# Low parts of u in half-tile loads, one more stored low part, and the first half's closing additions interleaved by bank

## The chip, the cores and the metric

One core of a Trainium2 chip runs the whole kernel in one launch. The metric is device time in microseconds (us), as the median of the runs; a profiled execution gives the trace that is read here. The core has a matrix engine (PE, with its weight loads PEld), a vector engine (DVE), an activation engine (ACT), a general engine (POOL) and a sync engine (SP). SP, ACT and POOL also issue DMA transfers, each into its own queue (q1, q10 and q0 in the profile), and each engine takes its instructions strictly in order.

## What is computed

A decoder layer over 256 tokens of width 2048, in float32. The change touches only the last stage, the feed-forward block:

```python
h = _rmsnorm(x, norm_mlp_pre[layer])
u = jnp.square(jax.nn.relu(h @ w_up[layer]))               # 256 x 8192
x = x + _rmsnorm(u @ w_down[layer], norm_mlp_post[layer])  # w_down: 8192 x 2048
```

## The kernel before

**Precision.** A float32 product is made of three PE products. Each operand is split into a high part (a rounded copy, made by ACT, `hi`) and a low part (the rest, made by DVE, `lo`); the products hi·hi, lo·hi and hi·lo are added up in PSUM (`three`, line 1031). Each weight tile of 128x1024 thus comes by a DMA into `raw` (5 buffers), is split by ACT (line 306) and DVE (line 307) into `hi` and `lo`, and is then used by PE. The class `Weights` runs this up to six tiles ahead of PE.

**The up and the down product.** `w_up` is taken in 8 chunks of 1024 columns; each leaves two groups of u, `uT[0]` to `uT[15]`, transposed, 128x1024 each (four slices of 128 rows of u's inner dimension, times 256 tokens). The down product takes `w_down` in two halves of 1024 columns, `c` = 0 and 1 (the first and the second half), and runs through all 16 groups `g` of u in each. Its inner dimension counts 64 slices `k`, or 32 pairs `kp` of slices; group g covers kp = 2g and 2g+1. A pair is done either as two plain steps (4 blocks of y times 3 parts per slice: 24 PE products, 5.4 us) or, for the pairs in `DOWN_SEVEN`, as seven block products in place of eight (7 times 3 parts: 21 PE products, 4.8 us): kp = 5, 7, 9, 11, 15, 17, 19, 21, 25, 27, 29 in the first half, and 3, 5, ... 27 in the second.

**Pair loads.** A pair with seven products needs sums of weight blocks. Its two weight slices come as one transfer of 1 MB that POOL issues (line 374) into `ab_down`, `c` or `u01`, in turn; DVE then adds blocks into `st_down` (lines 361, 365, 366), and ACT and DVE split the four tiles. I call this transfer the *pair load* of kp. In DVE's order these three additions stand ahead of the splits of the plain pair before, so a late pair load holds those back too.

**The low part of u.** u is used twice, and its low part is not kept in SBUF. After a group is finished, `lo_away` writes minus its rounded copy (`neg`) to DRAM by two ACT transfers into `ukeep[g]`, and later POOL issues two transfers of 256 KB that add u to it in DRAM (line 967, `ukeep<-u`, `accum_op=OP.add`), which leaves the low part there. `split_u` fetches it by one POOL transfer of 512 KB per group (line 979, `ulo<-ukeep`) into one of two buffers, issued after the first step of the group before, and makes the high part `uhi` on ACT. Group 0 has no stored low part: DVE makes it in both halves (line 981).

**The order of work.** There is no scheduler at run time. `Flow` keeps an estimated PE clock while the program is written out; generators such as `lo_away` and `half_evac` are resumed when that clock has passed the time that their last `yield` asked for, and this fixes where their instructions stand in each engine's order. POOL's queue therefore holds, in a fixed order, `ulo` loads, pair loads, the adding transfers and the reloads of sums of u (`s<-skeep`); a `ulo` load that waits until PE has finished with its buffer stops all that stand behind it.

**Closing the first half.** After the first half, `more` (in `c`) is added to each of four PSUM banks (`y`), ACT takes the sum of squares of the bank (`square`, `junkd`), and DVE writes the bank times the gain into `c` (line 1197). `half_evac` (line 1188) does this bank by bank during the first pairs of the second half, interleaved with DVE's splits. The banks are then reused as `md` by the seven-product pairs of the second half.

Of the kernel before, what the change touches and what calls it, by code (L numbers as in the profile page):

```python
# [26 lines left out]
P = 128  # L27
# [236 lines left out]
def layer(nc, tc, io):  # L264
# [49 lines left out]
    def tok(t, k, b):  # L314
        return t[:, k, b * P:(b + 1) * P]
# [617 lines left out]
    def up_evac(j, b, i, acc, order):  # L933
# [15 lines left out]
        nc.scalar.activation(uT[j][:, :, b * P:(b + 1) * P], t.rearrange("p (k s) -> p k s", k=4), AF.Square)  # L949
        if b and j:  # L950
            flow.start(lo_away(j), 2.0 + 4.0 * (j % 2))

    def lo_away(g):

        ukeep[g] = dram.tile([P, CW], F32, name=f"ukeep{g}")
        u = uT[g].rearrange("p k s -> p (k s)")
        for h in range(2):
            c = slice(h * 512, (h + 1) * 512)
            t = late["up"].tile([P, 512], F32, tag="r", bufs=2, name=f"neg{g}_{h}")
            nc.scalar.activation(t.bitcast(F32R), u[:, c], AF.Copy, scale=-1.0)  # L960
            yield 1.0
            nc.scalar.dma_start(out=ukeep[g][:, c], in_=t)
            yield 7.0
        yield 16.0
        for h in range(2):
            c = slice(h * 512, (h + 1) * 512)
            nc.gpsimd.dma_start(out=ukeep[g][:, c], in_=u[:, c], accum_op=OP.add)
            yield 2.0

    def split_u(c, g):  # L970
        if (c, g) == (0, 0):
            uh, ul = [wp.tile([P, CW], F32R, tag=w, bufs=W_BUFS, name=f"u{w}0").rearrange("p (k s) -> p k s", k=4)
                      for w in ("hi", "lo")]
        else:
            uh, ul = [dpl["dp"].tile([P, 4, S], F32R, tag=f"u{w}", bufs=2, name=f"u{w}{c}_{g}") for w in ("hi", "lo")]
        u, h, l = [x.rearrange("p k s -> p (k s)") for x in (uT[g], uh, ul)]
        if g:
            nc.scalar.activation(h, u, AF.Copy)
            nc.gpsimd.dma_start(out=l.bitcast(F32), in_=ukeep[g])
        else:  # L980
            split(h, l, u)
        return uh, ul

# [151 lines left out]
    def down_mm(c, u, k, b, n, w, first, last):  # L1135
        three(y[b][2 * c + n], [tok(u[x], k % 4, b) for x in range(2)], [t[:, 0, n * 512:n * 512 + 512] for t in w],
              first, last)
# [50 lines left out]
    def half_evac(more, g_half):  # L1188

        for n in range(2):  # L1190
            for b in range(NB):
                tt, out = nc.vector.tensor_tensor, more[b, n]
                tt(out=y[b][n], in0=y[b][n], in1=out, op=OP.add)
                yield 1.0
                square(n, b)
                yg[n, b] = out
                tt(out=out, in0=y[b][n], in1=g_half[n], op=OP.mult)
                yield 1.0

# [12 lines left out]
    for c in range(2):  # L1212
# [5 lines left out]
        for t, (what, k, tiles) in enumerate(wide_d[c]):  # L1218
# [10 lines left out]
            else:  # L1229
                if k == ws[0]:  # L1230
# [4 lines left out]
                    m = {i: bank(4 * (1 - c) + o, f"md{i}_{c}") for o, i in enumerate((1, 6, 7, 5))}  # L1235
                blocks = [[tok(u[x], 2 * (k % 2) + kk, bb) for x in range(2)] for kk, bb in ((0, 0), (1, 0), (1, 1))]
# [22 lines left out]
    for g in (GT - 2, GT - 1):  # L1259
        for b, n in PARTS:  # L1260
            for kk in range(4):
# [4 lines left out]
                else:  # L1266
                    three_more(y[b][2 + n], [tok(us[1, g][x], kk, b) for x in range(2)],
                               [t[:, 0, n * 512:n * 512 + 512] for t in w])
# [52 lines left out]
```

## Time and profile before

| what | value |
|---|---|
| median of 3 runs | 1049.46 us (1048.84 to 1049.66) |
| profiled execution, its own time | 1049.74 us |
| its span, first to last instruction | 1047.9 us, granted PE clock 0.998 |
| PE / DVE / ACT / POOL busy | 1035.3 / 834.0 / 644.5 / 90.4 us |
| down product in the trace | 703 to 1040 us; second half from 871 us |
| HBM traffic | 222.16 MB read, 25.17 MB written |

The profiled execution lies 0.28 us above the median of the runs. A busy PE is modelled, so its idle time is read from the starts of its products: undisturbed, one starts 0.227 us after the other. In the timelines each row has the start, the duration, the engine and line, and in square brackets how long the engine idled before it and what ended that.

### The profile page before, as it was taken

Reading aid. Unit: us, or ns where it says so; the run is one execution under the profiler, and the core shown is the slowest. Engines: PE = TensorE matmul, PEld = TensorE weight load, DVE = VectorE, ACT = ScalarE, POOL = GpSimd, SP = SyncE. Lnnn points to the kernel's source line nnn. Section 1 sums busy time; section 2 is a strip of 40 time slices with the busy share of each in tenths; the row PEclk is TensorE's granted clock in tenths of the full one; section 3 lists DMA queues with packets and bytes.
Section 4 is the critical chain, followed back from the end, with each engine's and each line's share of the span. In section 5 each row is a group of like instructions: output and inputs, shape, how many; then the busy total and the mean of one; then the engine's idle time right before and its main releaser. Section 6 shows DMA issues by size and latency. Waiting matters only on the chain.

```text
span 1047.9 us, 13455 instructions
## 1 busy us (share of the span) xinstructions
PE 1035.3 (99%) x4828; PEld 860.3 (82%) x4828; DVE 834.0 (80%) x1122; ACT 644.5 (62%) x884; POOL 90.4 (9%) x134
## 2 busy tenths in 40 slices
PE   9999999999999999999999999999999999999996
PEld 6888889888888788888888888788888888788785
DVE  6676536567557669999999999796989888998895
ACT  6674436565555566675766767666757564866661
POOL 0000000000000000111101011011201001212100
PEclk9999999999999999999999999999999999999999
DMA  9975447454447295758879587589997977789862
GB/s 301 368 230 150 139 131 240 142 162 156 145 164 235 84 370 180 252 177 263 238 237 289 174 251 232 164 289 346 306 380 250 362 260 236 276 314 338 330 233 81
DMA packets 89395, 248.21 MB, mean 237 GB/s; under 512 B 7920, under 2 KB 12528, under 8 KB 88944
## 3 DMA queue, kind: packets, MB, share of 16 engines
q1 hardware_dynamic: 61984, 162.03, 45.9%
q0 software_dynamic: 22592, 77.08, 23.3%
q10 hardware_dynamic: 4752, 8.24, 2.2%
q8 instruction: 38, 0.62, 0.2%
q14 instruction: 29, 0.24, 0.1%
HBM read 222.16 MB, written 25.17 MB: 236 GB/s over the span
## 4 chain that ended last, share of the span: by engine, by line
PE 86%; DVE 6%; DMA 3%; issue 2%; ACT 2%; SPq 0%; POOL 0%; DVEq 0%; POOLq 0%; ACTq 0%
PE acc_u L296 21%; PE y L296 20%; PE acc_o L296 8%; PE m L296 6%; PE md L296 5%; PE acc_v L296 4%; PE acc_qk L296 4%; DVE lo L307 3%; PE acc_ckv L296 2%; PE acc_ukv L296 2%; PE acc_q L296 2%; PE acc_cq L296 2%; PE acc_k L296 2%; PE acc_uq L296 2%; PE rt L300 1%
## 5 line engine op out<-in xcount | busy, mean ns | idle before, releaser
L307 DVE TENSOR_TENSOR lo<-raw,hi 128x1024 fp32r<-128x1024 f32 (+3 forms) x207 | 233.5, 1149 | 81.8 <-ACT hi L306 81.1
L306 ACT ACTIVATE hi<-raw 128x1024 fp32r<-128x1024 f32 (+3 forms) x207 | 203.3, 996 | 67.4 <-DMA raw<-in_w_in 15.4
L296 PE MATMUL acc_u<-hi,hT_hi 128*128 128x512 f32 x356 | 141.7, 398 | 0.0
L296 PE MATMUL acc_u<-hi,hT_lo 128*128 128x512 f32 x356 | 139.2, 391 | 0.4 <-DVE hT_lo L307 0.4
L296 PE MATMUL acc_u<-lo,hT_hi 128*128 128x512 f32 x356 | 138.8, 390 | 0.0
L296 PE MATMUL y<-hi,ulo 128*128 128x512 f32 x352 | 137.1, 390 | 0.8 <-DMA ulo<-ukeep 0.8
L296 PE MATMUL y<-lo,uhi 128*128 128x512 f32 x352 | 137.1, 390 | 0.7 <-DVE lo L307 0.7
L296 PE MATMUL y<-hi,uhi 128*128 128x512 f32 x352 | 137.3, 390 | 0.0
L310 ACT ACTIVATE hi<-raw,gcol 128x1024 fp32r<-128x1024 f32 x74 | 83.0, 1147 | 31.9 <-DMA raw<-in_w_up 20.1
L311 DVE SCALAR_TENSOR_TENSOR lo<-raw,gcol,hi 128x1024 fp32r<-128x1024 f32 x74 | 92.4, 1278 | 11.1 <-ACT hi L310 11.0
L296 PEld LDWEIGHTS acc_u<-hi,hT_lo 128*128 128x128 f32 x356 | 66.8, 188 | 14.9 <-DVE hT_lo L307 0.8
L296 PEld LDWEIGHTS y<-hi,ulo 128*128 128x128 f32 x352 | 66.0, 188 | 15.0 <-DMA ulo<-ukeep 1.2
L296 PEld LDWEIGHTS y<-lo,uhi 128*128 128x128 f32 x352 | 66.1, 188 | 14.6 <-DVE lo L307 1.2
L296 PEld LDWEIGHTS acc_u<-lo,hT_hi 128*128 128x128 f32 x356 | 67.0, 188 | 13.0
L296 PEld LDWEIGHTS acc_u<-hi,hT_hi 128*128 128x128 f32 x356 | 66.9, 188 | 12.8
L296 PEld LDWEIGHTS y<-hi,uhi 128*128 128x128 f32 x352 | 66.1, 188 | 13.7
L306 ACT ACTIVATE hi<-u 128x1024 fp32r<-128x1024 f32 (+1 forms) x38 | 37.5, 990 | 47.6 <-DVE u L366 34.7
L307 DVE TENSOR_TENSOR lo<-st_down,hi 128x1024 fp32r<-128x1024 f32 x48 | 57.5, 1219 | 1.1 <-ACT hi L306 1.0
L296 PE MATMUL md<-hi,s 128*128 128x512 f32 x144 | 52.1, 389 | 0.0
L306 ACT ACTIVATE hi<-st_down 128x1024 fp32r<-128x1024 f32 x48 | 49.8, 1050 | 3.4 <-DVE st_down L366 2.9
L296 PE MATMUL acc_o<-hi,mixT_hi 128*128 128x512 f32 x128 | 51.8, 405 | 0.0
L296 PE MATMUL acc_o<-hi,mixT_lo 128*128 128x512 f32 x128 | 50.2, 392 | 0.0
(330 smaller groups left out, 2171.1 us busy)
## 6 DMA issues: line engine op xcount, KB each, us to landing
raw<-in_w_down SPq DMA_DIRECT2D x80, 512.0 KB, 6.1
raw<-in_w_up SPq DMA_DIRECT2D x76, 512.0 KB, 6.4
raw<-in_w_in SPq DMA_DIRECT2D x55, 512.0 KB, 5.1
ab<-in_w_up POOLq DMA_DIRECT2D x22, 1024.0 KB, 6.1
raw<-in_w_out SPq DMA_DIRECT2D x32, 512.0 KB, 4.4
ulo<-ukeep POOLq DMA_DIRECT2D x30, 512.0 KB, 6.7
ab_down<-in_w_down POOLq DMA_DIRECT2D x13, 1024.0 KB, 9.2
ukeep<-neg ACTq DMA_DIRECT2D x30, 256.0 KB, 4.4
```

What stands on the lines that cost most here:

```text
L296: nc.tensor.matmul(out, a, b, start=start, stop=stop)
L300: nc.tensor.transpose(out, a, ident)
L306: nc.scalar.activation(hi, src, AF.Copy)
L307: nc.vector.tensor_tensor(out=lo, in0=src, in1=hi.bitcast(F32), op=OP.subtract)
L310: nc.scalar.activation(hi, src, AF.Copy, scale=g)
L311: nc.vector.scalar_tensor_tensor(out=lo, in0=src, scalar=g, in1=hi.bitcast(F32), op0=OP.mult, op1=OP.subtract)
```

## The change

1. `lo_away` is started for group 0 too, so that its low part is stored; in the second half it is loaded in place of DVE's subtraction. In the first half group 0 is split on DVE as before.
2. The wait between the `neg` stores and the adding transfers is 34 us of the estimated clock in place of 16, so these stand later in POOL's order.
3. The low part is loaded in halves of 256 KB, each for one pair, into four buffers of half the size; the half for pair kp+3 is issued after pair kp is written out (a plain pair: after its first step).
4. `half_evac` writes the gain multiplication of one bank after the addition of the next one, instead of right after its own.

```diff
-        if b and j:
+        if b:
             flow.start(lo_away(j), 2.0 + 4.0 * (j % 2))
...
-        yield 16.0
+        yield 34.0
         for h in range(2):
...
+        uh = dpl["dp"].tile([P, 4, S], F32R, tag="uhi", bufs=2, name=f"uhi{c}_{g}")
+        nc.scalar.activation(uh.rearrange("p k s -> p (k s)"), uT[g].rearrange("p k s -> p (k s)"), AF.Copy)
+        load_lo(2 * (c * GT + g) + 1)
+        return uh, [u_lo.pop(2 * (c * GT + g) + h) for h in range(2)]
+
+    u_lo = {}
+    next_lo = [2]
+
+    def load_lo(upto):
+
+        for i in range(next_lo[0], min(upto + 1, 4 * GT)):
+            g, h = i // 2 % GT, i % 2
+            t = u_lo[i] = dpl["dp"].tile([P, 2, S], F32R, tag="ulo", bufs=4, name=f"ulo{i}")
+            nc.gpsimd.dma_start(out=t.rearrange("p k s -> p (k s)").bitcast(F32), in_=ukeep[g][:, h * 512:(h + 1) * 512])
+            next_lo[0] = i + 1
...
+        def half_gain(b, n):
+            yg[n, b] = more[b, n]
+            nc.vector.tensor_tensor(out=more[b, n], in0=y[b][n], in1=g_half[n], op=OP.mult)
+
+        done = []
         for n in range(2):
             for b in range(NB):
-                tt, out = nc.vector.tensor_tensor, more[b, n]
-                tt(out=y[b][n], in0=y[b][n], in1=out, op=OP.add)
+                nc.vector.tensor_tensor(out=y[b][n], in0=y[b][n], in1=more[b, n], op=OP.add)
+                square(n, b)
                 yield 1.0
-                square(n, b)
-                yg[n, b] = out
-                tt(out=out, in0=y[b][n], in1=g_half[n], op=OP.mult)
-                yield 1.0
+                if done:
+                    half_gain(*done.pop())
+                    yield 1.0
+                done.append((b, n))
+        half_gain(*done.pop())
...
+            load_lo(2 * c * GT + (k if what == "w" else k // 2) + 3)
             nxt = (c, g + 1) if g < GT - 1 else (1, 0)
```

PE's and SP's orders do not change. POOL's order at the start of the down product, before: the number behind `ukeep` and the last one of `ulo0_1` is the group; the two `ab_down` rows are the pair loads of kp 5 and 9, and the `c` row is that of kp 7.

```order
L979 DMA ulo0_1_6408<-ukeep1_3831 128x1024
L967 DMA ukeep12_6087<-ab_3502 128x512
L374 DMA ab_down_6373<-in_w_down 128x2x1024
L967 DMA ukeep12_6087<-ab_3502 128x512
L967 DMA ukeep13_6161<-ab_3502 128x512 x2
L979 DMA ulo0_2_6529<-ukeep2_4169 128x1024
L374 DMA c_3504<-in_w_down 128x2x1024
L979 DMA ulo0_3_6616<-ukeep3_4236 128x1024
L374 DMA ab_down_6373<-in_w_down 128x2x1024
L979 DMA ulo0_4_6712<-ukeep4_4553 128x1024
```

The same place in the changed kernel; `ulo6` is now the half of pair kp 6.

```order
L374 DMA ab_down_6382<-in_w_down 128x2x1024
L989 DMA ulo4_6485<-ukeep2_4174 128x512
L989 DMA ulo5_6537<-ukeep2_4174 128x512
L989 DMA ulo6_6580<-ukeep3_4241 128x512
L967 DMA ukeep12_6093<-ab_3502 128x512
L374 DMA c_3504<-in_w_down 128x2x1024
L967 DMA ukeep12_6093<-ab_3502 128x512
L989 DMA ulo7_6628<-ukeep3_4241 128x512
L967 DMA ukeep13_6166<-ab_3502 128x512 x2
L989 DMA ulo8_6704<-ukeep4_4559 128x512
L374 DMA ab_down_6382<-in_w_down 128x2x1024
L989 DMA ulo9_6728<-ukeep4_4559 128x512
```

The adding transfers of groups 12 and 13 have moved from ahead of and between the first pair loads to around the second; the pair load of kp 7 now stands behind `ulo6`, whose buffer is the one of pair 2, and that of kp 9 behind `ulo8`, whose buffer is that of pair 4.

POOL's order in the middle of the second half, before (the pair loads of kp 23, `ab_down`, and 25, `u01`):

```order
L404 DMA s1_21_8584<-skeep21_7396 128x1024
L979 DMA ulo1_10_8605<-ukeep10_5706 128x1024
L374 DMA ab_down_6373<-in_w_down 128x2x1024
L979 DMA ulo1_11_8692<-ukeep11_5778 128x1024
L374 DMA u01_3505<-in_w_down 128x2x1024
```

And in the changed kernel, from the pair load of kp 21 on; in the second half the half of pair kp is `ulo` 32+kp:

```order
L374 DMA u01_3505<-in_w_down 128x2x1024
L404 DMA s1_21_8645<-skeep21_7427 128x1024
L989 DMA ulo53_8665<-ukeep10_5712 128x512
L989 DMA ulo54_8730<-ukeep11_5783 128x512
L374 DMA ab_down_6382<-in_w_down 128x2x1024
L989 DMA ulo55_8754<-ukeep11_5783 128x512
L989 DMA ulo56_8819<-ukeep12_6093 128x512
L374 DMA u01_3505<-in_w_down 128x2x1024
```

A half (`ulo54`) now stands between the other half and the pair load of kp 23, and it waits for the buffer of pair 18, that is for PE, where the whole load ahead of it waited only for pair 17.

DVE's order where the first half is closed, before (`y00` is the bank of tokens 0 to 127 and columns 0 to 511, `y10` of tokens 128 to 255; `u01` at the end is the pair load of kp 5):

```order
L1193 TENSOR_TENSOR y00_6374<-y00_6374,c_3504 128x512
L1197 TENSOR_TENSOR c_3504<-y00_6374,g_half0_7240 128x512
L307 TENSOR_TENSOR lo394_7849<-ab_down_6373,hi394_7848 128x1024
L1193 TENSOR_TENSOR y10_6376<-y10_6376,c_3504 128x512
L1197 TENSOR_TENSOR c_3504<-y10_6376,g_half0_7240 128x512
L307 TENSOR_TENSOR lo395_7869<-st_down_6372,hi395_7868 128x1024
L1193 TENSOR_TENSOR y01_6375<-y01_6375,c_3504 128x512
L1197 TENSOR_TENSOR c_3504<-y01_6375,g_half1_7241 128x512
L307 TENSOR_TENSOR lo396_7889<-st_down_6372,hi396_7888 128x1024
L1193 TENSOR_TENSOR y11_6377<-y11_6377,c_3504 128x512
L1197 TENSOR_TENSOR c_3504<-y11_6377,g_half1_7241 128x512
L361 TENSOR_TENSOR st_down_6372<-u01_3505 128x1024
```

And in the changed kernel:

```order
L1208 TENSOR_TENSOR y00_6383<-y00_6383,c_3504 128x512
L1208 TENSOR_TENSOR y10_6385<-y10_6385,c_3504 128x512
L307 TENSOR_TENSOR lo394_7894<-ab_down_6382,hi394_7893 128x1024
L1203 TENSOR_TENSOR c_3504<-y00_6383,g_half0_7269 128x512
L1208 TENSOR_TENSOR y01_6384<-y01_6384,c_3504 128x512
L307 TENSOR_TENSOR lo395_7914<-st_down_6381,hi395_7913 128x1024
L1203 TENSOR_TENSOR c_3504<-y10_6385,g_half0_7269 128x512
L1208 TENSOR_TENSOR y11_6386<-y11_6386,c_3504 128x512
L307 TENSOR_TENSOR lo396_7936<-st_down_6381,hi396_7935 128x1024
L1203 TENSOR_TENSOR c_3504<-y01_6384,g_half1_7270 128x512
L1203 TENSOR_TENSOR c_3504<-y11_6386,g_half1_7270 128x512
L361 TENSOR_TENSOR st_down_6381<-u01_3505 128x1024
```

Each gain multiplication has moved behind the split that follows its bank's addition. On ACT the `junkd` of `y10` moves up with it: ACT now has both `junkd` of `y00` and `y10` ahead of `uhi` and of the `hi` of that split, and one `junkd` ahead of the `hi` of each of the two after it, as before. DVE's subtraction for the low part of group 0 (`ulo<-u01`), a few rows above, is gone.

More of the change, by code (lines that the diff above doesn't have):

```diff
@@ L971, in split_u, with utok @@
         if (c, g) == (0, 0):
[L972 to L982, printed above, removed]
+            uh, ul = [wp.tile([P, CW], F32R, tag=w, bufs=W_BUFS, name=f"u{w}0") for w in ("hi", "lo")]
+            split(uh, ul, uT[0].rearrange("p k s -> p (k s)"))
+            uh, ul = [x.rearrange("p (k s) -> p k s", k=4) for x in (uh, ul)]
+            return uh, [ul[:, 0:2], ul[:, 2:4]]
+        uh = dpl["dp"].tile([P, 4, S], F32R, tag="uhi", bufs=2, name=f"uhi{c}_{g}")
[10 more added lines that the diff above has]
+            next_lo[0] = i + 1
+    def utok(u, x, k, b):
+        return tok(u[1][k // 2], k % 2, b) if x else tok(u[0], k, b)
     def keep_s(kp):
@@ L1135, in down_mm @@
     def down_mm(c, u, k, b, n, w, first, last):
-        three(y[b][2 * c + n], [tok(u[x], k % 4, b) for x in range(2)], [t[:, 0, n * 512:n * 512 + 512] for t in w],
+        three(y[b][2 * c + n], [utok(u, x, k % 4, b) for x in range(2)], [t[:, 0, n * 512:n * 512 + 512] for t in w],
               first, last)
```

4 lines of the change are left out of this document (2 added, 2 removed).

## Prediction

> **What bounds the kernel now.** I read the page's first part, then PE's waits, then PE's timeline around the two waits that lie in the down product.
>
> ```profile
> span 1047.9 us, 13455 instructions
> ...
> PE 1035.3 (99%) x4828; PEld 860.3 (82%) x4828; DVE 834.0 (80%) x1122; ACT 644.5 (62%) x884; POOL 90.4 (9%) x134
> ```
> ```profile
> PE y L296 <- DMA ulo<-ukeep: 0.8, 1, 0.8
> PE y L296 <- DVE lo L307: 0.7, 1, 0.7
> ```
> ```profile
> 892.91 0.39 PE L296 MATMUL y<-hi,uhi 128*128 128x512 f32 x1
> 894.04 0.50 PE L296 MATMUL y<-lo,uhi 128*128 128x512 f32 x1 [0.74 <-DVE lo L307]
> ...
> 975.79 0.39 PE L296 MATMUL y<-lo,uhi 128*128 128x512 f32 x1
> 976.98 0.50 PE L296 MATMUL y<-hi,ulo 128*128 128x512 f32 x1 [0.80 <-DMA ulo<-ukeep]
> ```
>
> PE is busy 99% of the span, and its own order doesn't change, so the change can win only time in which PE waits. In the stage that it touches that is two gaps. Products follow each other in 0.227 us, so the first gap costs 894.04 - 892.91 - 0.23 = 0.90 us, the second 976.98 - 975.79 - 0.23 = 0.96 us. All that can be won is about 1.9 us, which is 0.18%. A measurement of this kernel tells about 0.2% (2.1 us) from no change. What can be lost isn't bounded so; it hangs on how close behind DVE and the transfers stand elsewhere.
>
> **The gap at 977: low parts in halves.** This load came late because its queue was full when it was issued.
>
> ```profile
> 966.37 0.53 POOL L979 DMA_DIRECT2D ulo<-ukeep  x1
> 966.89 0.70 POOL L374 DMA_DIRECT2D ab_down<-in_w_down  x1
> ```
>
> Issued at 966.4, used at 976.0 at the earliest: 9.6 us of lead. In the changed kernel a half waits for the buffer of the pair four before, so three pairs of 4.8 or 5.4 us lie between issue and use, some 15 us. The load at 966.4 landed some 10.6 us after its issue (PE waited for it until 976.98). With 15 us of lead and half the bytes I count the gap as gone: **-0.96 us** (at worst it stays: 0).
>
> **The gap at 894: the interleaved closing.** DVE's timeline first, then ACT's.
>
> ```profile
> 868.06 1.22 DVE L307 TENSOR_TENSOR ulo<-u,uhi 128x1024 fp32r<-128x1024 f32 x1
> ...
> 876.39 0.69 DVE L1193 TENSOR_TENSOR y<-y,c 128x512 f32<-128x512 f32 x1
> ...
> 880.87 0.69 DVE L1193 TENSOR_TENSOR y<-y,c 128x512 f32<-128x512 f32 x1
> 882.38 0.69 DVE L1197 TENSOR_TENSOR c<-y,g_half 128x512 f32<-128x512 f32 x1 [0.81 <-ACT junkd L1145]
> 883.33 1.22 DVE L307 TENSOR_TENSOR lo<-st_down,hi 128x1024 fp32r<-128x1024 f32 x1 [0.26 <-ACT hi L306]
> 884.47 0.69 DVE L1193 TENSOR_TENSOR y<-y,c 128x512 f32<-128x512 f32 x1
> ...
> 890.18 1.22 DVE L361 TENSOR_TENSOR st_down<-u 128x1024 f32<-128x1024 f32 x1
> ...
> 892.77 2.35 DVE L307 TENSOR_TENSOR lo<-raw,hi 128x1024 fp32r<-128x1024 f32 x2
> ```
> ```profile
> 877.12 0.60 ACT L1145 ACTIVATE junkd<-y 128x512 bf16<-128x512 f32 x1 [6.08 <-DVE y L1193]
> ...
> 878.65 1.05 ACT L306 ACTIVATE hi<-ab_down 128x1024 fp32r<-128x1024 f32 x1
> ...
> 881.66 0.60 ACT L1145 ACTIVATE junkd<-y 128x512 bf16<-128x512 f32 x1 [1.96 <-DVE y L1193]
> ...
> 882.24 1.05 ACT L306 ACTIVATE hi<-st_down 128x1024 fp32r<-128x1024 f32 x1
> ```
>
> The tile that PE waits for is the first `lo` of the row at 892.77. Before it DVE and ACT take turns, one round from 880.87 to 884.47, 3.60 us: addition, then ACT's `junkd` 0.79 after the addition's start, ACT's `hi` 0.58 later, DVE's `lo` 1.09 later, and the next addition 1.14 later. The gain multiplication at 882.38 waits 0.81 us for `junkd`, which looks like the loss to be removed; but DVE could not go on before `hi` anyway. The multiplication lies in the shadow of that wait, and only 0.26 us of wait stands behind it. In the new order it stands behind the `lo`, on DVE's path. I rebuild the sequence with these steps (0.60 from one 128x512 step's start to the next, as from 889.58 to 890.18 in the last round), from the first addition at 0: second addition 0.6; `junkd` 0.73 and 1.33; `uhi` 1.91; `hi` 2.86 (`junkd` to `hi` over `uhi` is 1.53 above); `lo` 3.94; multiplication 5.08; addition 5.68; `junkd` 6.41; `hi` 6.99; `lo` 8.07; multiplication 9.21; addition 9.81; `junkd` 10.54; `hi` 11.12; `lo` 12.20; multiplications 13.34 and 13.94; `st_down` 14.54. Before, that was 890.18 - 876.39 = 13.79, so the new order is **0.75 us longer**. Against it stands the subtraction at 868.06, 1.14 us to the next start, that is taken off DVE ahead of it; but the pair load of kp 3 now stands behind a half that waits for pair 29 of the first half (PE ends it at 861.2), and takes 8 to 9 us, so its data come at about 869.5 to 870.7, against 869.8 when DVE would be ready. The start moves 0.2 to 1.1 us earlier. Net for the gap: -0.4 to +0.5; I take **0**: the gap stays. The banks' reuse by `md` isn't late: the multiplication of the second bank that PE needs (at 890.41) ends at about 889.3 to 890.2.
>
> **The pair loads behind the halves.** This is what the change adds, and what the two gaps don't show. Queues and load first, then the places.
>
> ```profile
> q1 hardware_dynamic: 61984, 162.03, 45.9%
> q0 software_dynamic: 22592, 77.08, 23.3%
> q10 hardware_dynamic: 4752, 8.24, 2.2%
> ```
> ```profile
> ab_down<-in_w_down POOLq DMA_DIRECT2D x13, 1024.0 KB, 9.2
> ...
> c<-in_w_down POOLq DMA_DIRECT2D x5, 1024.0 KB, 12.8
> ```
> ```profile
> 705.00:735.00 30.00, 30.00 (x141) 24.61 (x140) 19.74 (x26) 20.64 (x30) 6.00 (x9) 1.00 0.99 335
> 731.70:757.80 26.10, 26.10 (x116) 21.59 (x116) 25.69 (x31) 18.14 (x23) 6.48 (x9) 1.00 1.00 315
> ...
> 955.00:980.00 25.00, 24.20 (x107) 19.74 (x106) 19.85 (x23) 15.56 (x18) 4.76 (x8) 1.00 1.01 386
> ```
> ```profile
> 707.67 2.08 POOL L374 DMA_DIRECT2D c<-in_w_down  x1
> ...
> 728.00 0.70 POOL L374 DMA_DIRECT2D ab_down<-in_w_down  x1
> ```
> ```profile
> 721.77 0.39 PE L296 MATMUL y<-lo,uhi 128*128 128x512 f32 x1
> ...
> 757.81 0.39 PE L296 MATMUL y<-lo,uhi 128*128 128x512 f32 x1
> ```
> ```profile
> 731.68 1.23 DVE L361 TENSOR_TENSOR st_down<-c 128x1024 f32<-128x1024 f32 x1 [2.10 <-DMA c<-in_w_down]
> ...
> 742.32 1.23 DVE L361 TENSOR_TENSOR st_down<-ab_down 128x1024 f32<-128x1024 f32 x1
> ...
> 755.54 2.35 DVE L307 TENSOR_TENSOR lo<-raw,hi 128x1024 fp32r<-128x1024 f32 x2
> ```
>
> From 731.68 to 757.8 DVE works 25.69 of 26.10 us (third column of the windows), so a delay at 731.68 or 742.32 goes through to the `lo` at 755.54. The first of its two ends at 756.76, and PE uses it at 757.81: 1.05 us of slack. The engines of the DMA are full over the same stretch (0.99 and 1.00, the column before the last).
>
> Pair 7: its load was issued at 707.67 and DVE waited for it until 731.68. Now it stands behind `ulo6`, which waits until PE leaves pair 2, at 721.8 (the first products with the next weights). With `ulo6` and one adding transfer ahead it is issued at about 723. It lands between 8.5 and 12.8 us later, nearer the low end since the adding transfers and itself no longer crowd the queue before 722: about 732.5, 1 us late. Pair 9: issued at 728.00 before, now behind `ulo8`, which waits for pair 4, 5.4 + 5.4 us after 721.8, thus at about 733.5. Alone it would land 9.2 us later, at 742.7. But three adding transfers are still ahead. Of q0's 77.08 MB, 7.9 are adding transfers (30 of 256 KB); the other 69.2 MB at q1's rate (162.03 MB in 45.9% of 1047.9 us) would take 205 us, and q0 took 244, so one costs 39/30 = 1.3 us. That makes 742.7 to 746.6; in the middle 744.3, 2.0 us after DVE asks for it at 742.3. Past the slack, PE loses **0.9 us** (0, if the loads land as early as before; 3.2 if all three are in front).
>
> The Trainium skill speaks against halves: DMA: Bandwidth & Descriptors, "Anatomy of one DMA", fits 2.0 us plus bytes/436e3 per transfer on POOL's path. By it a half is an estimated 2.6 us, a whole 3.2; if the fixed part held the queue, two halves would cost 2.0 us more than one whole, the pair load behind them would come that much later, and the term would be 2.9. The trace disagrees as to holding: q10, which is nearly all 256 KB transfers, moved 8.24 MB in 2.2% of the span, 357 GB/s, where q1 has 337.
>
> Later pair loads in both halves are issued about 5 us later as well, since each stands behind a half that waits for the middle of a group. Where a `lo` tile follows such a load between 790 and 960, read in the same way, DVE has it ready some 3 us or more ahead of PE, so I count nothing there, with up to 1 us open at pair 17, where the last adding transfers now lie. In the second half the tight place is pair 23:
>
> ```profile
> 982.00 1.23 DVE L361 TENSOR_TENSOR st_down<-ab_down 128x1024 f32<-128x1024 f32 x1 [3.40 <-DMA ab_down<-in_w_down]
> ...
> 984.60 2.35 DVE L307 TENSOR_TENSOR lo<-raw,hi 128x1024 fp32r<-128x1024 f32 x2
> ```
> ```profile
> 987.09 0.39 PE L296 MATMUL y<-lo,uhi 128*128 128x512 f32 x1
> ```
>
> The load of 966.89 came at 982, and the first `lo` behind it was ready at 985.82, 1.27 us ahead of PE. Without the gap at 977 PE comes 0.96 earlier: 0.3 us are left. The load is now issued behind pair 18, at about 971.6. At 8.3 to 9.2 us it would land by 981; but the queues are full until 980 (1.01), and pair 21's load, 5 us later too, has kept DVE back. I take sums 0 to 1.2 us later: **+0.4 us** (0 to 0.9).
>
> **Edits that cost nothing.** Four ACT instructions and two adding transfers for group 0, in chunk 1: `lo` is there 5 us and more ahead of PE. Some 40 more issues on POOL, 0.5 us each: POOL is busy 9%. The later adding transfers in the other chunks: nobody reads them before the down product.
>
> **Sum.** -0.96 + 0 + 0.9 + 0.4 = +0.3 us. The profiled execution took 1049.74 us, so 1050.0; it lies 0.28 above the median of the runs, thus 1049.8 us.
>
> **Rivals.** (a) Forecast: gains and new waits cancel, 1048.5 to 1051.5; chance 0.56. (b) Slower: in the first half the pair loads of 7 and 9 come 4 us late or more, because the adding transfers are drained in front of them while the queue was idle before 722. It decides from a delay of 3.2 us on (1.05 slack plus the gains); with 4 to 6 us late PE loses 3 to 5, and the time is 1051.9 to 1054. For it speaks the DMA share of 1.00 over the stretch, against it that q0 loses four adding transfers ahead of pair 5's load, so that DVE is earlier there. Chance 0.24. (c) Faster: both gaps close and pair loads land as before, -1.9, or 1047.5; for it speaks that the same bytes move in all, against it the rebuilt sequence. Chance 0.15. (d) A half holds the queue for longer than its bytes. At the 1.3 us of an adding transfer of the same size, in place of 0.78 at q1's rate, two halves are 1.0 us longer than one whole, the loads of pairs 9 and 23 come that much later, and 2.0 more makes 1051.8. Against it stands q10's rate. Chance 0.05. The Trainium skill's fit (DMA: Bandwidth & Descriptors, "Anatomy of one DMA") would have it, with 2.0 us per two halves; q10's row does not. That the change doesn't do what it says can be left out: the orders show all of it.
>
> **Range and chances.** From (c) to the lower part of (b): 1047.4 to 1052.8 us. Faster by over 0.2%: 0.11, the part of (c) that finds a little more than the two gaps. Slower: 0.25, from (b) and half of (d). Same: 0.64.
>
> **What would show it.** PE's waits: no `ulo` any more; a wait of `y` on DVE `lo` near 894 still, of 0.5 to 1.4 us; one near 747 to 758, and one near 986. DVE's timeline: from the first `y<-y,c` to the `st_down<-u` 14.5 us in place of 13.79, with no wait on `junkd` but longer ones on ACT `hi`; `st_down<-c` of pair 7 after 732 with a longer wait, and `st_down<-ab_down` of pair 9 waiting for its load. POOL: the pair loads of 7 and 9 at 723 and 733.5. I am wrong if pair loads still land ahead of DVE (then (c)), or if PE waits for `lo` by more than 3 us between 737 and 790 (then (b)).

## The result, and the profile after

The change makes the kernel slower: 1062.58 us median (1061.89 to 1064.39, four runs) against 1049.56 (1048.84 to 1050.17) for the kernel before on the same chip, a ratio of 1.0127 (95% interval 1.0109 to 1.0145). The forecast was 1049.8, with a range up to 1052.8.

The first part of the page of after, then PE's waits (us in total, times, longest):

```profile
span 1061.1 us, 13521 instructions
...
PE 1039.0 (98%) x4828; PEld 861.1 (81%) x4828; DVE 831.9 (78%) x1121; ACT 645.0 (61%) x886; POOL 109.9 (10%) x168
```
```profile
PE y L296 <- DVE lo L307: 8.6, 4, 5.2
PE rt L300 <- ACT r L937: 1.8, 2, 1.4
...
PE md L296 <- ACT uhi L977: 1.2, 1, 1.2
```

The wait for `ulo` is gone, as forecast; PE's wait for DVE's `lo` went from 0.7 to 8.6 us, and one single wait of 5.2 us makes most of it. PE's timeline there, and the windows around it (busy times of PE, PEld, DVE, ACT and POOL, then the granted clock of PE and the share of the DMA):

```profile
797.98 0.79 PE L296 MATMUL y<-lo,uhi 128*128 128x512 f32 x1 [5.21 <-DVE lo L307]
798.57 0.63 PE L296 MATMUL y<-hi,ulo 128*128 128x512 f32 x1
...
803.26 0.54 PE L296 MATMUL y<-lo,uhi 128*128 128x512 f32 x1
803.64 0.40 PE L296 MATMUL y<-hi,ulo 128*128 128x512 f32 x1
```
```profile
750.00:790.00 40.00, 39.30 (x172) 32.23 (x173) 32.50 (x40) 23.52 (x27) 9.60 (x14) 1.00 0.86 283
790.00:800.00 10.00, 4.79 (x18) 3.60 (x17) 5.82 (x7) 2.63 (x3) 0.55 (x1) 0.84 0.88 339
800.00:810.00 10.00, 10.00 (x38) 8.07 (x37) 9.83 (x13) 6.84 (x8) 1.43 (x3) 0.82 0.63 183
```

Two losses lie on top of each other. PE stands still for 5.4 us; and after that its clock is down (0.84 and 0.82 in place of 1.00), so that the next 12 products follow each other in some 0.43 us and not in 0.227 us. PE looks busy all the while (10.00 of 10.00 from 800 to 810, with 38 products where the kernel before has 46). This is pair 16's place, which the kernel before passed at 789.09. What PE waits for stands in DVE's order behind pair 17's sums; these wait for pair 17's load, and that one for POOL's queue. POOL's timeline, then DVE's:

```profile
770.94 1.80 POOL L967 DMA_DIRECT2D ukeep<-uT  x2
777.21 0.57 POOL L989 DMA_DIRECT2D ulo<-ukeep  x1 [4.47 <-PE y L296]
777.77 0.89 POOL L967 DMA_DIRECT2D ukeep<-uT  x1
778.32 1.08 POOL L374 DMA_DIRECT2D c<-in_w_down  x1
```
```profile
794.11 1.22 DVE L361 TENSOR_TENSOR st_down<-c 128x1024 f32<-128x1024 f32 x1 [11.24 <-DMA c<-in_w_down]
```

The pair load (`c`) is issued at 778.32, right behind a half that waited for PE and behind the adding transfers of groups 14 and 15, and DVE waits 11.24 us for it. In the kernel before the same load went out at 768.14:

```profile
768.14 0.70 POOL L374 DMA_DIRECT2D c<-in_w_down  x1
```

So it is issued 10.2 us later, of which some 3.3 us are earlier waits of PE in this execution, and from issue to landing it takes 15.7 us in place of 13.0. The other new waits of PE are between 0.3 and 1.7 us; the largest in the down product are:

```profile
750.57 0.50 PE L296 MATMUL y<-lo,uhi 128*128 128x512 f32 x1 [1.51 <-DVE lo L307]
```
```profile
903.16 0.47 PE L296 MATMUL md<-hi,s 128*128 128x512 f32 x1 [1.18 <-ACT uhi L977]
...
907.39 0.50 PE L296 MATMUL y<-lo,uhi 128*128 128x512 f32 x1 [1.01 <-DVE lo L307]
```
```profile
1000.39 0.50 PE L296 MATMUL y<-lo,uhi 128*128 128x512 f32 x1 [0.90 <-DVE lo L307]
```

From start to start, less 0.227 us, the gaps add up to the loss:

| place in after | before | after | difference |
|---|---|---|---|
| 670 and 712, `rt<-r` | 0.81 | 1.57 + 0.54 | +1.3 |
| 751 and 761, pairs 8 and 10 (behind the loads of 9 and 11) | 0 | 1.67 + 0.30 | +2.0 |
| 798, pair 16 (behind pair 17's load) | 0 | 5.37 + 0.36 | +5.7 |
| 799 to 804, 12 slow products | 0 | 2.35 | +2.4 |
| 903, `md`, end of the closing | 0 | 1.34 | +1.3 |
| 907, first `lo` after the closing | 0.90 | 1.17 | +0.3 |
| `ulo` at 977 in before | 0.96 | 0 | -1.0 |
| 1000, pair 23's place | 0 | 1.06 | +1.1 |
| sum (spans: 1061.1 - 1047.9 = 13.2) | | | 13.1 |

### The profile page after: what moved, and what is told of

It reads as the page before. It is cut to its first block, busy times and chain, and to the rows that moved or that the text cites. A ratio compares the mean times of both kernels' runs of the same rounds, so it can differ in the third digit from the quotient of the medians.

```text
span 1061.1 us, 13521 instructions
## 1 busy us (share of the span) xinstructions
PE 1039.0 (98%) x4828; PEld 861.1 (81%) x4828; DVE 831.9 (78%) x1121; ACT 645.0 (61%) x886; POOL 109.9 (10%) x168
## 4 chain that ended last, share of the span: by engine, by line
PE 77%; DVE 7%; DMA 7%; issue 6%; POOL 1%; ACT 1%; SPq 0%; DVEq 0%; POOLq 0%; ACTq 0%
PE acc_u L296 21%; PE y L296 13%; PE acc_o L296 8%; PE m L296 6%; PE acc_v L296 4%; PE acc_qk L296 4%; PE md L296 3%; DMA ab_down<-in_w_down 3%; DVE lo L307 3%; PE acc_ckv L296 2%; PE acc_q L296 2%; PE acc_ukv L296 2%; PE acc_cq L296 2%; PE acc_k L296 2%; PE acc_uq L296 2%
## 5 line engine op out<-in xcount | busy, mean ns | idle before, releaser
L989 POOL DMA_DIRECT2D ulo<-ukeep x62 | 33.9, 547 | 279.4 <-PE md L296 132.4
```

The costliest lines, as they stand in the source:

```text
L989: nc.gpsimd.dma_start(out=t.rearrange("p k s -> p (k s)").bitcast(F32), in_=ukeep[g][:, h * 512:(h + 1) * 512])
```

## The experiments

My theory after this reading was *stacking*: pair 17's load is made late twice, by the adding transfers in front of it and by the half that it stands behind, and PE pays once the sum is past the slack. Its rivals: the adding transfers alone, or the halves alone. A third question was what the small waits belong to. Ratios are to the kernel before, run on the same chip.

**The four parts, one by one.** First the later adding transfers alone.

```diff
-        yield 16.0
+        yield 34.0
```

> The kernel before with one number changed: lo_away pauses 34.0 in place of 16.0, so the adding transfers of groups 12 to 15 stand later in POOL's order, those of 14 and 15 directly ahead of pair 17's load; low parts still in whole tiles, closing as before, u0 by DVE. Stacking (my theory: pair 17's load is made late twice, by the adding transfers in front of it and by the half that it stands behind, and only the sum uses up the slack of 2.95 us): four transfers of 1.3 us each are 5.2 us, less the slack 2.3 us, and some of that comes back because earlier loads are relieved: 1049.5 to 1053, with a wait for lo near 789 of 0 to 3 us. Transfers alone: the wait is the 5 us of the changed kernel and the slow products stand behind it: 1056 to 1059. Halves alone: no change, 1049.5.

Measured: 1054.39 us, ratio 1.0033 (1.0021 to 1.0045). DVE's row for pair 17 and PE's rows:

```profile
789.88 1.23 DVE L361 TENSOR_TENSOR st_down<-c 128x1024 f32<-128x1024 f32 x1 [9.00 <-DMA c<-in_w_down]
```
```profile
793.75 0.50 PE L296 MATMUL y<-lo,uhi 128*128 128x512 f32 x1 [2.30 <-DVE lo L307]
...
795.56 0.63 PE L296 MATMUL y<-lo,uhi 128*128 128x512 f32 x1
```

Three adding transfers now stand right in front of the load, and from issue to landing it takes 18.1 us in place of 13.0. So these transfers, part 2 of the change, cost PE a wait of 2.46 us and seven slow products, from 795 to 798; the prediction had priced them at nothing. A wait of 0 to 3 us is what stacking had let expect; the slow products behind it were not in its sum. The slack in the expectation is too small by 1.1 us: it was read to the end of two splits, and PE needs the first.

Then the halves alone: `load_lo` and `utok` as in the change, the pause at 16.0, the closing as before, and u0's low part subtracted by DVE in two pieces.

> The kernel before with the low parts in half tiles and the lead of three pairs as the only edit; group 0's low part in the second half is still subtracted by DVE, in two pieces of 512; adding transfers early, closing as before. Stacking: waits of 0 to 2 us near 750, 0 to 2 near 789 and about 1 near 986, the gap at 977 gone: 1050 to 1053. Halves alone: a wait of about 5 us near 789 and slow products behind it: 1057 to 1060. If halves are harmless once the rest is undone: 1048.5.

Measured: 1052.07 us, ratio 1.0019 (1.0009 to 1.0028). No wait at pair 16, though DVE waits longer for pair 17 than in before (the row below). The loss lies elsewhere, in 0.3 us each near 750 and 760, 2.04 near 898 and 1.02 near 991:

```profile
786.89 1.23 DVE L361 TENSOR_TENSOR st_down<-c 128x1024 f32<-128x1024 f32 x1 [4.79 <-DMA c<-in_w_down]
```

In this execution ACT waits 3.56 us for a plain weight tile at 864.73, and against PE's products the closing starts 1.1 us later than in before, as much as the gap of 0.90 has grown. Why that tile came late isn't shown.

The closing alone (the edit of `half_evac` in the change, the rest as before):

> The kernel before with the interleaved closing as the only edit. If the wait of md<-hi,s at 903 in the changed kernel comes from the gain multiplications, which now leave the first bank one step later: DVE's sequence is 0.75 to 1 us longer, PE waits for md some 1 to 1.4 us near 890 and about 1 us at 894: 1050.5 to 1051.5. If the closing is harmless and that wait has another cause (u0 or the pair load): 1049.5, no wait for md. If it helps: 1048.6, the gap at 894 gone.

Measured: 1050.85 us, ratio 1.0002 (0.9993 to 1.0012), no measurable change. Its waits were of the expected kind, but the one for `md` is small: 0.34, and 1.15 for `lo` in place of 0.90.

```profile
877.81 1.29 DVE L1197 TENSOR_TENSOR y<-y,c 128x512 f32<-128x512 f32 x2
...
892.61 1.22 DVE L361 TENSOR_TENSOR st_down<-u 128x1024 f32<-128x1024 f32 x1
```

From 877.81 to 892.61 are 14.80 us, where the kernel before took 13.79 and the rebuilt sequence 14.54.

Group 0's low part alone:

```diff
-        if b and j:
+        if b:
...
-        if g:
+        if (c, g) != (0, 0):
```

> The kernel before with u0's low part stored in chunk 1 and loaded in the second half, in a whole tile like the others; nothing else. DVE loses one subtraction of 1.14 us ahead of the closing. If DVE sets the start of the closing, the gap near 894 (0.90) goes: ratio 0.9985 to 0.9995. If the pair load of pair 3 sets it, or the added load delays that one: the gap stays at 0.9 to 2: 1.000 to 1.0015.

Measured: 1053.01 us, ratio 1.0025 (1.0016 to 1.0035), slower than either end of the expectation. DVE is rid of 1.14 us of work, and PE's gap at this place grows from 0.90 to 2.32 us. POOL in before, then POOL, DVE and PE in this run:

```profile
850.60 0.70 POOL L374 DMA_DIRECT2D ab_down<-in_w_down  x1 [0.22 <-issue]
```
```profile
861.78 0.53 POOL L979 DMA_DIRECT2D ulo<-ukeep  x1 [9.67 <-PE y L296]
862.30 0.70 POOL L374 DMA_DIRECT2D ab_down<-in_w_down  x1
```
```profile
874.91 1.23 DVE L361 TENSOR_TENSOR st_down<-ab_down 128x1024 f32<-128x1024 f32 x1 [5.57 <-DMA ab_down<-in_w_down]
```
```profile
898.03 0.50 PE L296 MATMUL y<-lo,uhi 128*128 128x512 f32 x1 [2.05 <-DVE lo L307]
```

The added load waits for its buffer until PE leaves it, and pair 3's load behind it goes out at 862.30 in place of 850.60. DVE starts 4.0 us later (874.91 against 870.94) and not 1.1 earlier; PE is 1.7 us later itself in this execution, so some 2.3 us of that count. It is the same mechanism, once more in POOL's queue.

**Two parts together** (the halves of the second run with the pause of the first):

> The kernel before with two parts of the change: halves asked for three pairs ahead, and the pause of lo_away at 34.0; the closing and u0 as before. Alone the halves gave a ratio of 1.0019 and the later transfers 1.0033. If the two delays of pair 17's load only add up in the time: 1.005. Stacking (each is half hidden by the slack of pair 17's tile alone, together nothing hides them, and the longer wait brings more slow products): a wait of 4.5 to 5.5 us near 795 with 8 or more products at 0.43 us behind it, ratio 1.007 to 1.010.

Measured: 1062.40 us, ratio 1.0112 (1.0093 to 1.0131). That is a little above the range expected for stacking. These two parts make nearly the whole 1.0127, while the two alone gave 1.0033 and 1.0019.

```profile
795.05 1.22 DVE L361 TENSOR_TENSOR st_down<-c 128x1024 f32<-128x1024 f32 x1 [11.25 <-DMA c<-in_w_down]
```
```profile
798.92 0.80 PE L296 MATMUL y<-lo,uhi 128*128 128x512 f32 x1 [5.23 <-DVE lo L307]
```

Now the arithmetic can be seen. In before DVE waits 2.70 us for this load, and the first `lo` behind it is ready 4.1 us ahead of PE:

```profile
781.20 1.23 DVE L361 TENSOR_TENSOR st_down<-c 128x1024 f32<-128x1024 f32 x1 [2.70 <-DMA c<-in_w_down]
...
783.79 1.22 DVE L307 TENSOR_TENSOR lo<-raw,hi 128x1024 fp32r<-128x1024 f32 x1
```
```profile
789.09 0.39 PE L296 MATMUL y<-lo,uhi 128*128 128x512 f32 x1
```

DVE's waits beyond 2.70 are 2.09 with the halves, 6.30 with the later transfers, and 8.55 with both: they add up (2.09 + 6.30 = 8.39). PE's waits should be these less the slack of 4.1 us: none, 2.2 and 4.5; measured are 0, 2.46 and 5.39, the last 0.9 more than this simple account gives. DVE's delays add up; PE's loss isn't, because the slack is spent once, and the slow products come on top (10 of them here, 2.0 us).

**The changed kernel with one thing undone.** The pause at 16.0 again:

> The changed kernel with the pause of lo_away at 16.0 again; halves, u0's low part by transfer and the interleaved closing stay. Stacking: the wait of 5.2 us near 798 shrinks to under 1 us and with it the 13 products at 427 ns go, which were some 2.7 us: 1062.6 - 8 = 1054.6, between 1051.5 and 1056, the rest being the waits near 750, 903, 907 and 1000. Transfers alone: 1049 to 1051. Halves alone: the wait stays, 1060 to 1063.

Measured: 1053.51 us, ratio 1.0035 (1.0021 to 1.0049). The wait at 798 and its slow products are gone, 0 us there. What stays are the small waits, 1.65 us for `md`, 1.16 behind it, and 0.72 and 0.73 further on.

Halves two pairs ahead in place of three, with the late transfers:

```diff
-            load_lo(2 * c * GT + (k if what == "w" else k // 2) + 3)
+            load_lo(2 * c * GT + (k if what == "w" else k // 2) + 2)
```

> The changed kernel with the halves asked for two pairs ahead in place of three; the four parts of the change otherwise stay. In POOL's order the halves then go out in twos, and each pair load stands behind halves that wait for the same pair as the whole tile did before; pair 17's still has the last four adding transfers in front. Stacking (two delays of pair 17's load, one from the adding transfers, one from the half): only the first is left, as in the run with late transfers alone: a wait of 2 to 3 us near 790 with up to 1.5 us of slow products, none near 750 and 761: 1054 to 1057. If the transfers alone made the wait, it stays above 4.5 us: 1059 to 1062. If the halves' number and not their place made it: 1060 to 1063.

Measured: 1054.21 us, ratio 1.0041 (1.0027 to 1.0055). The wait at pair 16 is 1.74 us with no slow products behind it; those at 751, 761 and 1000 are gone (0.25 and 0.27 us at 803 and 814 are new). One number in the code, which sets the place of the halves among the pair loads, is worth more than 8 us.

The last four adding transfers later still, behind pair 21's load and in front of the next one, which is pair 25's (the expectation calls it 23's):

```diff
-        yield 34.0
+        yield 34.0 if g < 14 else 70.0
```

> The changed kernel with the pause of lo_away at 70.0 for groups 14 and 15 (34.0 for the others): their four adding transfers stand later still, behind pair 21's load and in front of pair 23's. If what costs is their place directly in front of pair 17's load, the wait near 798 and its slow products go, 8 us, and a smaller wait of 0 to 3 us may come near 822 at pair 23, whose tile has some 3 us of slack: 1052 to 1057. If it is the late time of these transfers as such, the wait stays or moves with them: 1059 to 1064.

Measured: 1056.44 us, ratio 1.0063 (1.0049 to 1.0077). No wait near 798 any more; so it is not their late time but their place in front of pair 17's load. Pair 25's tile took them without a wait of PE. The time isn't lower, among other things because the wait near 751 is 2.24 us here, with six slow products behind it; why it is longer than in after (1.67) isn't shown.

The halves two pairs ahead and nothing else of the change:

> The kernel before with low parts in half tiles, asked for two pairs ahead; adding transfers early, DVE subtracts u0's low part in the second half, closing as before. If halves cost only by where the pair loads stand behind them: no wait near 750, 789 and 986 that was not there, and the first half of a group still comes 5 us earlier than the whole tile did, so the 0.96 us gap at 977 goes: ratio 0.998 to 1.000. If two small transfers hold the queue longer than one (the rival on the sum, 1.0 to 2.0 us per pair of halves), waits come back where loads are tight: 1.001 to 1.003, as with three pairs ahead.

Measured: 1050.28 us, ratio 0.9999 (0.9990 to 1.0008). In its profile PE waits nowhere in the second half, neither for `ulo` nor near 894; two small halves in place of one whole cost nothing. The time isn't lower, since this execution has gaps of 0.31, 1.58 and 0.66 us at 664, 670 and 712, ahead of the down product's tight places.

**What doesn't belong to the change.** The kernel before, profiled once more:

> The kernel before, unchanged, profiled once more. If the waits of rt<-r near 670 (1.57 us in the changed kernel and in every experiment, 0.81 in the first profile of before) and near 712 belong to the change, they are 0.8 and 0 here; if they vary from execution to execution or chip to chip, one or both show up here as well.

Measured: 1050.53 us. The wait at 670 is 1.43 us here too, the gap near 894 is 1.06, and the wait for `ulo` at 977 isn't there. So +0.6 us of the table's first row are the execution's, not the change's; whether the 0.5 at 712 is, stays open (of 0.4 to 0.8 us at this step in six of the runs here, 3.7 in one whose cause is told below, and absent in the others). The `ulo` gap at 977 is the execution's as well. Six other profiles in this document are of kernels that load the low part whole; at this product five of them have a gap of 0.1 us or none, and one of 0.32 us. So the -1.0 in the table isn't shown to be a gain of the halves.

**Which queue.** What stayed open was whether it is the order in POOL's queue, or the traffic on the DMA engines. Pair 17's load alone was issued from SP:

```diff
-            return load_two(raw, nc.gpsimd, io["w_down"][...])
+            return load_two(raw, nc.sync if (c, kp) == (0, 17) else nc.gpsimd, io["w_down"][...])
```

> The changed kernel, all four parts, with pair 17's load alone issued from SP's queue in place of POOL's; there it stands behind the store of s_11, which the changed kernel issued near 770. If the place in POOL's order is the cause, the load goes out near 770 in place of 778.3 and lands by 785, the wait of 5.4 us near 798 shrinks below 1.5 us and its slow products go: 1062.6 - 7 = 1055.5 us, between 1053.5 and 1057. If the traffic of the adding transfers is the cause, the load lands near 790 all the same, and 1059 to 1063 us remain.

Measured: 1058.95 us (1056.56 to 1059.23), ratio 1.0075 (1.0057 to 1.0093), between the two expectations. In the profiled execution, the fastest of the four, the place is clean; SP, then DVE:

```profile
768.43 0.39 SPq L374 DMA_DIRECT2D c<-in_w_down  x1
```
```profile
783.00 1.23 DVE L361 TENSOR_TENSOR st_down<-c 128x1024 f32<-128x1024 f32 x1
```

Issued ten microseconds earlier, with the same bytes in the other queues, the load is there when DVE comes to it: no wait at all in place of 11.24. From issue to landing it takes 12.6 us in place of 15.7, among the same adding transfers. So ten of the thirteen microseconds come from the time of issue, which POOL's order sets, and three from the way behind it; whether those three are the place in POOL's queue or the kind of queue isn't separated. Traffic alone didn't keep the load until 790. What made the other three runs 2.4 us longer than the profiled one isn't shown.

All pair loads of the down product on SP:

> The changed kernel with every pair load of the down product on SP's queue, so that none stands behind a half or an adding transfer. If the order of POOL's queue is the cause of the other waits too (near 750, 761 and 1000 from the pair loads, near 907 from pair 3's load behind u0's halves), these go as well; what is left is the closing's wait for md of about 1 us: 1049.5 to 1052. If SP's queue is worse for them (the weights behind a pair load wait until its buffer is free), weights come late in new places: above 1054.

Measured: 1053.33 us, ratio 1.0025 (1.0011 to 1.0039). The time lies between the two expectations. All waits of the down product that the change had brought are gone, the one for `md` too, which the expectation had left in; and one of a new kind has come, in ACT's rows and then PE's:

```profile
715.50 1.06 ACT L306 ACTIVATE hi<-raw 128x1024 fp32r<-128x1024 f32 x1 [3.79 <-DMA raw<-in_w_down]
```
```profile
717.67 1.12 PE L300 MATMUL rt<-ident,r 128*128 128x128 f32 x4 [3.55 <-ACT r L937]
```

Pair 5's load now stands ahead of weights in SP's queue that are needed first. With that one back on POOL (`nc.gpsimd if (c, kp) == (0, 5) else nc.sync`):

> As the run with all pair loads on SP, with pair 5's back on POOL, where it stands behind two halves that wait for nothing late. If the wait at 717 (3.72 us and 1.0 us of slow products) came from that load alone, it goes; since that wait also gave the later loads more lead, up to 2 us of the waits near 897 may come back: 1047.5 to 1050, ratio 0.997 to 1.000. If pair 7's load, then ahead of the weights asked for at 708, does the same harm: 1051 to 1054.

Measured: 1048.87 us (1048.03 to 1049.85), ratio **0.9983** (0.9974 to 0.9991). This version is faster than the changed kernel by 1.4%, and than the kernel before by 0.17%; the interval leaves out 1, but the margin is small. PE's waits in it, the longest ones:

```profile
PE rt L300 <- ACT r L937: 1.8, 2, 1.4
PE warm L521 <- DVE zero L518: 1.2, 1, 1.2
```

In the down product's own steps PE waits no more, with all four parts of the change inside; what is left there is the `rt` step at 712.

With pair 7's load on POOL as well:

> As the run before, with pair 7's load on POOL as well, behind the half that waits until PE leaves pair 2; adding transfers late, as in the change. If pair 7's load hurts the weights on SP, this one is the faster of the two: 1048 to 1050.5. If its place on POOL is the worse one, the wait near 740 of the run with pair 17 alone on SP (1.4 us) is back: 1050.5 to 1052.5.

Measured: 1056.17 us, ratio 1.0048 (1.0034 to 1.0061), in the direction of the second expectation and over three times its size. One load in the wrong place is a wait of 4.97 us with ten slow products behind it:

```profile
743.27 0.79 PE L296 MATMUL y<-lo,uhi 128*128 128x512 f32 x1 [4.81 <-DVE lo L307]
```

**What a wait costs behind itself.** Two runs made PE wait on purpose.

```diff
+        for i in range(1 + full):
             nc.vector.tensor_tensor(out=lo, in0=src, in1=hi.bitcast(F32), op=OP.subtract)
+        for i in range(half):
+            nc.vector.tensor_tensor(out=lo[:, :512], in0=src[:, :512], in1=hi[:, :512].bitcast(F32), op=OP.subtract)
```

> The kernel before with subtractions of DVE done again in five places of the up product, one per chunk, where the tile has 3.3 us of slack before PE: additional DVE time of 5.2, 5.7, 6.3, 6.8 and 7.4 us makes PE wait some 1.8, 2.4, 3.0, 3.5 and 4.1 us near 482, 526, 572, 618 and 665. If a wait only costs itself, all products behind are 0.227 us apart. If a long wait lowers the clock, products of 0.427 us follow from some length on; with the wait of 2.46 us in the run with late transfers followed by 7 such, and 2.04 in the run with halves by none, from about 2.3 us on, and more of them the longer the wait, up to some 13.

> As the run before, with the lengths in another order over the same five places (3.5, 1.8, 4.1, 2.4 and 3.0 us expected), so that length and place can be told apart. If the length alone decides, the same lengths give the same number of slow products; if it hangs on the moment (a window of the clock that runs by itself), the same length gives different numbers.

Measured, with the gap, the number of products at some 0.43 us behind it, and what these lost beyond 0.227 us each:

| place | first run | second run |
|---|---|---|
| 484 | 2.51: 8, 1.55 us | 4.31: 12, 2.40 us |
| 533 | 3.04: 5, 1.00 us | 2.51: 7, 1.40 us |
| 584 | 3.77: 11, 2.20 us | 5.03: 10, 2.00 us |
| 633 | 4.30: 13, 2.56 us | 3.05: 8, 1.62 us |
| 684 | 4.97: 13, 2.59 us | 3.72: 7, 1.40 us |

Each wait was 0.6 to 0.9 us longer than planned. The granted clock of the first run's first and last place (third column from the end):

```profile
480.00:490.00 10.00, 7.50 (x25) 5.35 (x25) 9.90 (x10) 3.84 (x5) 0.85 (x1) 0.83 0.90 238
...
681.00:692.00 11.00, 7.43 (x20) 5.83 (x21) 10.90 (x11) 1.16 (x3) 0.00 (x0) 0.69 0.87 201
```

All ten were followed by slow products. The number grows with the length only loosely: waits of 3.7 us gave 7 and 11. Against that, 1.74 (lead of two), 1.97 (`md`, pair 17 on SP), 2.04 (halves alone) and 2.32 us (u0 alone) gave none, and 2.24 us (transfers later still) gave six. So from somewhere around 2.3 us on a wait costs 1.0 to 2.6 us more than itself here.

## Why the prediction was wrong

- **The step that failed** is "with up to 1 us open at pair 17, where the last adding transfers now lie", counted as nothing. It measured 5.7 us of wait and 2.4 us of slow products, 8.1 of the 13.1 us lost. The numbers to size it were in the text: four adding transfers of 1.3 us each ahead of the load are 5.2 us, and the load was to be issued some 5 us later besides, behind its half. Against the slack (3 us in the text, 4.1 by the rows above) these are a wait of several microseconds. Alone, the later transfers cost PE 2.46 us of wait at this place and the halves nothing; together they cost 5.39 us, and slow products came on top. I had looked for the danger at pairs 7 and 9, where DVE has next to no slack, and let the slack of pair 17 stand for an answer without adding up what would be set against it.
- **"The later adding transfers in the other chunks: nobody reads them before the down product"** names the wrong cover. Nobody waits for them; but they stand in a queue, and what stands behind them is waited for. Alone they gave a ratio of 1.0033.
- **The rivals.** (b) had the mechanism, adding transfers in front of a pair load, and its form, with a point from which it decides; but at pairs 7 and 9, and at most 5 us. Its sign, a wait of more than 3 us between 737 and 790, came at 789 in the times of before, but for pair 17's load. Its place was wrong, and no rival held the clock's part. (d), the halves holding the queue, is refuted by the halves two pairs ahead, 0.9999, with no wait in the tight places. The prediction had set it aside by the rate of q10, which is ACT's queue and not POOL's; so that reason didn't bear on it. The Trainium skill's fit for one transfer (DMA: Bandwidth & Descriptors, "Anatomy of one DMA") gives (d) only if its fixed part is read as a time that the queue is held; that section itself puts most of that part after the data, on the wait for the write to be confirmed, and 0.9999 agrees with this.
- **Right, in kind:** pairs 7 and 9, +0.9 (0 to 3.2), measured +1.67; their loads went out at 724.39 and 734.74 (forecast 723 and 733.5), and DVE waited for both, 6.18 and 2.50 us. The middle of the prediction's 742.7 to 746.6 is 744.65, not 744.3, so its own term was +1.3. The 0.30 at 761, behind pair 11's load, had been counted as nothing. Pair 23, +0.4 (0 to 0.9), measured +1.06, just out of its range. The length of the rebuilt closing, 14.54 us, measured 14.79 (888.74 to 903.53) in after.
- **Luck:** the `ulo` gap at 977 went, but of the six other profiles with whole loads none has more than 0.32 us there. The term of -0.96 rested on one execution.
- **The closing, net 0** (-0.4 to 0.5) measured +1.6. The late `lo` was +0.3 of it. The rest, 1.34, is a wait that the prediction had weighed and called not late: the gain multiplication reads the PSUM bank, the new order does it one round later, and `md` takes over that bank. The profile blames ACT's `uhi`; but the product reads `hi` and `s` and not `uhi`, and with the old closing `md` products ran before that `uhi` was made, and one waited for DVE's gain row instead, as PE's timeline of the run with u0 alone shows (`uhi` was ready at 895.4 there). In after `md` starts 0.83 us after the first of the two last gains, as in the five other runs with this wait (0.83 or 0.84); `uhi` ends within 0.04 us of that gain in all of them, so this figure by itself doesn't tell the two apart.

```profile
894.32 0.50 PE L296 MATMUL md<-hi,s 128*128 128x512 f32 x1 [0.20 <-DVE c L1197]
```

Of the 1.34 us only 0.34 are the new order by itself, as in the run with the closing alone. There the closing's first addition (877.81) starts 13.86 us before the product ahead of `md` (891.67); in after it is 12.86 us (888.74 to 901.60), one microsecond less, and the wait is one microsecond longer. With the pair loads on SP it starts 16.96 us ahead (874.96 to 891.92, pair 5's load on POOL), and the wait is gone. So the prediction's start, 0.2 to 1.1 us earlier, is wrong too: against the same product of PE it came 0.7 us later than in before (13.57 us, 876.39 to 889.96). DVE waited for pair 3's load, which stood behind a half that waited for PE until 871.68:

```profile
883.28 1.23 DVE L361 TENSOR_TENSOR st_down<-ab_down 128x1024 f32<-128x1024 f32 x1 [0.93 <-DMA ab_down<-in_w_down]
```

- **"Four ACT instructions and two adding transfers for group 0"** cost nothing, but the load that goes with them did: alone, a ratio of 1.0025. I had its effect on pair 3 at 8 to 9 us after an issue behind PE; alone it took 12.6.

## What to carry to other kernels

An engine that only issues transfers can look idle (POOL 9%) and still be the tightest order in the kernel: before moving a transfer, list what stands behind it in its queue, with each one's slack, and add up all delays of the change at one load before comparing the sum with the slack. A transfer that waits for a buffer should not stand ahead of one whose data are needed soon; here the place of a single load was worth 4 to 7 us (pairs 5, 7 and 17), and moving all pair loads but one to another queue turned a loss of 1.3% into a gain of 0.17%. Small gaps of a microsecond are a poor prize: they came and went from one execution of the same kernel to the next.

## What was new about the hardware

After a wait of PE of some 2.3 us or more the products behind it started 0.43 us apart in place of 0.227 us for 2 to 6 us, and the granted clock in the 10 or 11 us around it fell to 0.66 to 0.84. In after this was 2.4 us on top of 5.7. The Trainium skill (TensorE: Matmul & The Clock Gate, "HAM oscillation — how this bites in real kernels") gives the rule of no idle gaps above some 3.4 us; here 2.24, 2.46 and 2.51 us were enough, so the measured bound is lower. The same page of the Trainium skill ("What's actually happening") has the clock set by how busy PE was in a window that runs by itself. The runs fit such a window but don't prove it: waits of nearly the same length (3.72 and 3.77 us) gave 7 and 11 slow products, and waits of 2.24 and 2.32 us gave six and none.
